# Moving the place of the split weights in SBUF: larger tiles with a start that steps by 64 bytes, one raw buffer fewer

## The chip, the core and the metric

The kernel runs on one core of one Trainium2 chip, and the time is device microseconds of one execution. Three executions of the kernel before gave 1087.91, 1085.91 and 1089.38 us, so the median is 1087.91 us. A fourth execution was taken with the hardware profiler, and all rows below are from it.

## What is computed

Two layers of a hybrid block over 256 positions of width 1024, in float32. In each layer a normed input goes through one wide projection, whose columns feed three things: an attention that picks 64 keys per query with an index score, a state-space scan (with a causal convolution ahead of it and a grouped norm behind it), and two gates. The two branches are projected, gated, added, and projected once more. Then comes a feed-forward layer with a short convolution.

```python
def reference(x, ...):
    for l in range(DEPTH):
        h = rms_norm(x, norm_mix_w[l])
        x = x + hybrid_mixer(h, w_in[l], ...)
        h = rms_norm(x, norm_ffn_w[l])
        x = x + conv_glu_ffn(h, ffn_w_up[l], ...)
    return rms_norm(x, norm_final_w)

def hybrid_mixer(h, w_in, ...):
    proj = h @ w_in
    ...
    a = dsa_attention(q, k, v, qi, ki, wi)
    b = mamba2_branch(z, xbc, dt_raw, ...)
    merged = jax.nn.sigmoid(g_attn) * (a @ w_proj_attn) + jax.nn.sigmoid(g_ssd) * (b @ w_proj_ssd)
    return merged @ w_out

def conv_glu_ffn(h, w_up, conv_w, conv_b, w_down):
    u = causal_dwconv(h @ w_up, conv_w, conv_b)
    gate, val = u[..., :FFN_DIM], u[..., FFN_DIM:]
    return (jax.nn.silu(gate) * val) @ w_down
```

## The kernel before

**Chunks.** All weights come in 350 chunks of at most 128 partitions by 1024 float32 (512 KB). SyncE loads a chunk into one of `RAW_BUFS` = 5 tiles `raw` (L174). ScalarE rounds it to the type of TensorE's faster float32 product, `whi` (L199), and VectorE writes what is left over, `wlo = raw - whi` (L200). There are three pairs `whi`, `wlo` (`SPLIT_BUFS`). Some chunks are split early into tiles of activations that are not in use then; these are the tables `EARLY_FFN`, `EARLY_MIX` and `EARLY_CONV`, and the tiles are called `ebig`, `ehxh`, `ex`, `es`, `ez` and so on. `take` (L188) hands the split pair of the next chunk to the caller, and loads and splits ahead as far as buffers allow. A raw tile comes free when VectorE's subtraction has read it.

**Products.** Each activation is split in the same way, into a high and a low part. A chunk of 8 blocks of 128 x 128 takes 24 matmuls: for each block the weights' high part times the activation's high part (L370) and low part (L371), and then for each block the low part of the weights times the activation's high part (L376). The block of weights is the stationary operand, which a LDWEIGHTS reads from SBUF (512 bytes of each partition), and the activation is the moving operand (256 columns, 1024 bytes of each partition). `n_outer` does this for one output tile, `k_outer` for four at a time. L370, L371 and L376 have 2464 matmuls each, 7392 together. The first projection's index and query columns (L549 to L551) go the other way round: the activation is stationary and 308 or 512 columns of weights are moving.

```python
        for j, k in enumerate(ks):
            nc.tensor.matmul(ps, wh[:, j, :], hi(k), start=first and j == 0, stop=False)
            nc.tensor.matmul(ps, wh[:, j, :], lo(k), start=False, stop=False)
```

**Order.** Attention, scan and norms are generators in three lanes. `take` runs a step of them after a chunk. The order of the instructions on each engine is set by a scheduler that simulates a timeline, with loads and splits at high priority; so the count of raw tiles has a say in where it puts the other work.

**Places.** Tiles lie in SBUF in the order in which their pools meet them, so a tile's start is the sum of the widths ahead of it. Matmul operands step by 512 or 1024 bytes inside a tile, so the start of each, modulo 512 bytes, is that of its tile:

| tiles | start modulo 512, before |
|---|---|
| `raw`, `whi`, `wlo` | 64 |
| `uh`, `ul` (tags Bm, Cm, lg0, lg1), `bL` and `ebig` (tags big0, big1) | 64 |
| tags s0 to s3: `bH`, `es`, and the first two pairs of `fH`, `fL` | 384 |
| `hxh`, `hxl`, `mH`, `mL`, `ths`, tags x0 to x3, z0 to z3 (`aH`, `aL`, the other `fH`, `fL`, `ex`, `ez`) | 0 |

The step from 64 to 384 comes from `wd`, which is 320 bytes wide, and the step to 0 from `dec`, which is 128. I call the start of the weights' block minus the start of the activation, modulo 512, the **distance** of a matmul. In the program before, the 7392 matmuls of L370, L371 and L376 have these distances: 64 for 5808 of them (`hxh`, `hxl`, `mH`, `aH`, later `fH`, with `whi` and `wlo`), 192 for 896 (`bH`, first `fH` and `fL`), 448 for 288 and 320 for 96 (`uh` and `ul` with early chunks), 0 for 304 (`bL`, and `hxh` with an early chunk in `ex`).

Of the kernel before, what the change touches and what calls it, by code (L numbers as in the profile page):

```python
# [9 lines left out]
F32 = mybir.dt.float32  # L10
F32R = mybir.dt.float32r
# [7 lines left out]
P = 128  # L19
# [11 lines left out]
BIG = 1.0e30  # L31
TOPK = 64

RAW_BUFS = 5
SPLIT_BUFS = 3

FIRST_PAIRS = 4

# [24 lines left out]
def hybrid_kernel(ctx: ExitStack, tc: tile.TileContext, a: dict, out: bass.AP):  # L63
    nc = tc.nc

    const = ctx.enter_context(tc.tile_pool(name="const", bufs=1))
    wraw = ctx.enter_context(tc.tile_pool(name="wraw", bufs=RAW_BUFS))
    wsp = ctx.enter_context(tc.tile_pool(name="wsp", bufs=SPLIT_BUFS))
    act = ctx.enter_context(tc.tile_pool(name="act", bufs=1))
# [67 lines left out]
        make_early(base, EARLY_MIX)  # L137
        make_early(base + 20, EARLY_CONV)

    st = {"cur": 0, "prep": 0, "dma": 0, "now": 0, "mm": None}  # L140
    lanes = {"norm": [], "attn": [], "scan": []}

    def side(lane, gen, delay):
# [25 lines left out]
    def load_some():  # L169
        while st["dma"] < len(order) and st["dma"] < st["prep"] + RAW_BUFS:  # L170
            i = order[st["dma"]]
            src, b, c = chunks[i]
            r = wraw.tile([P, 8 * 128], F32, name="raw", tag="raw")
            nc.sync.dma_start(r[:, :b * c].rearrange("p (b c) -> p b c", b=b), src)  # L174
            raws[i] = r[:, :b * c]
            st["dma"] += 1

    def split_tiles(j):
        if j in early:
            t0, t1 = early[j]  # L180
            if t0 == t1:
                t = act.tile([P, 2, 8 * 128], F32R, name=f"e{t0}", tag=t0)
                return [t[:, 0], t[:, 1]]
            return [(tmp if t in ("Xt", "pT") else act).tile([P, 8 * 128], F32R, name=f"e{t}", tag=t, bufs=1)
                    for t in (t0, t1)]
        return [wsp.tile([P, 8 * 128], F32R, name=t, tag=t) for t in ("whi", "wlo")]

    def take():  # L188
        i = st["cur"]
        with tc.high_priority():  # L190
            load_some()
            while st["prep"] < len(order):
                j = order[st["prep"]]
                if j not in early and sum(k not in early for k in splits) == SPLIT_BUFS:
                    break
                src, b, c = chunks[j]
                hi, lo = (t[:, :b * c] for t in split_tiles(j))
                r = raws.pop(j)
                nc.scalar.copy(out=hi, in_=r)  # L199
                nc.vector.tensor_sub(lo, r, hi.bitcast(F32))  # L200
                splits[j] = [t.rearrange("p (b c) -> p b c", b=b) for t in (hi, lo)]
                st["prep"] += 1
                load_some()
        st["cur"] += 1
        if st["mm"] is not None:
            side_steps()
        return splits.pop(i)
# [197 lines left out]
    for l in range(L):  # L405

        tok = [act.tile([P, 8 * T], F32, name=f"big{t}", tag=f"big{t}")[:, :1856] for t in range(2)]
        V = [act.tile([P, T], F32, name=f"V{t}", tag=f"V{t}") for t in range(2)]
        wd = act.tile([P, 2, 40], F32, name="wd", tag="wd")

        def rotate(v, t, heads, dim, rot, o):
            h = rot // 2
# [83 lines left out]
        dA = act.tile([P, 2, 32], F32, name="dA", tag="dA")  # L496
        Pc = act.tile([P, 2, 32], F32, name="Pc", tag="Pc")
        nP = act.tile([P, 2, 32], F32, name="nP", tag="nP")
        dec = act.tile([P, 32], F32, name="dec", tag="dec")

        prd = dram.tile([32, 2, P], F32, name=f"prd{l}")

# [491 lines left out]
```

## Time and profile before

| | |
|---|---|
| median of three executions | 1087.91 us |
| their range | 1085.91 to 1089.38 us |
| the profiled execution's time | 1091.08 us |
| its span, first to last instruction | 1089.1 us |
| PE busy, LDWEIGHTS (PEld) busy | 1064.4 us (98%), 1026.2 us (94%) |
| VectorE, ScalarE, GpSimd busy | 877.9 us, 696.2 us, 66.5 us |
| mean granted TensorE clock, as a share of the full one | 0.997 |
| read from HBM | 189.26 MB, 175 GB/s over the span |

The span is what the instructions cover; the profiled execution's time is 2 us more. A matmul's recorded duration covers its way through the array and overlaps the next one's, so the time that it costs is read from start to start, which is called its pitch below, and not from its duration.

### The profile page before, as it was taken

The page shows a single profiled execution, that of the slowest core. Times are in us where ns is not written, and L with a number is a line of the kernel's source. Part 1 is how long each engine was busy: PE and PEld are TensorE (multiplying, and loading weights), DVE is VectorE, ACT ScalarE, POOL GpSimd, SP SyncE. Part 2 cuts the span into 40 slices and gives each one's busy share as a digit, 9 for nine tenths or more (in the row PEclk, how much of TensorE's full clock was granted, in tenths as well). Part 3 has the DMA queues.
Part 4 walks back from the last instruction along what each step waited for, and adds up shares of the span by engine and source line. Part 5 has one row for each costly group of instructions (what it writes and reads, how often), then busy time and mean ns, then how long its engine had stood idle before and what let it go on. Part 6 is the DMA issues. An engine that isn't in the chain of part 4 may idle for free.

```text
span 1089.1 us, 22471 instructions
## 1 busy us (share of the span) xinstructions
PE 1064.4 (98%) x8704; PEld 1026.2 (94%) x8704; DVE 877.9 (81%) x1755; ACT 696.2 (64%) x1285; POOL 66.5 (6%) x74
## 2 busy tenths in 40 slices
PE   6999999999999999998999999999999999999997
PEld 5789989999999999998997999999999999999997
DVE  6898988879877899885668999887887878888643
ACT  5658878647555576665555699865665556666552
POOL 3000000022000200000100000000310020000010
PEclk9999999999999999999999999999999999999999
DMA  7546444555677346666645654555567761666661
GB/s 266 183 148 213 151 147 156 161 169 175 194 233 251 117 122 195 194 199 211 183 134 176 224 155 139 164 172 155 175 190 216 246 216 45 182 187 191 180 182 48
DMA packets 52841, 191.82 MB, mean 176 GB/s; under 512 B 5952, under 2 KB 6240, under 8 KB 51712
## 3 DMA queue, kind: packets, MB, share of 16 engines
q1 hardware_dynamic: 50832, 180.31, 53.8%
q0 software_dynamic: 1472, 9.17, 2.3%
q8 instruction: 68, 1.11, 0.4%
q10 hardware_dynamic: 432, 0.92, 0.2%
q14 instruction: 37, 0.30, 0.1%
HBM read 189.26 MB, written 1.11 MB: 175 GB/s over the span
## 4 chain that ended last, share of the span: by engine, by line
PE 85%; DMA 5%; ACT 4%; DVE 3%; issue 2%; DVEq 0%; ACTq 0%; POOLq 0%
PE acc L370 23%; PE acc L371 23%; PE acc L376 23%; PE acc L550 3%; PE acc L551 2%; PE acc L549 2%; DMA bc<-prd 2%; DMA raw<-in_wu_dram 2%; PE sb L705 1%; DVE wlo L200 1%; ACT whi L199 1%; PE sa L461 1%; DVE ul L327 1%; PE sa L589 1%; PE sa L614 1%
## 5 line engine op out<-in xcount | busy, mean ns | idle before, releaser
L199 ACT CAST whi<-raw 128x1024 fp32r<-128x1024 f32 (+2 forms) x320 | 331.9, 1040 | 225.1 <-PE acc L371 168.7
L200 DVE TENSOR_TENSOR wlo<-raw,whi 128x1024 fp32r<-128x1024 f32 (+2 forms) x320 | 387.0, 1212 | 107.5 <-ACT whi L199 103.1
L370 PE MATMUL acc<-hxh,whi 128*128 128x256 f32 x1456 | 353.3, 282 | 1.0 <-ACT ths L657 0.9
L371 PE MATMUL acc<-hxl,whi 128*128 128x256 f32 x1456 | 351.2, 281 | 0.0
L370 PEld LDWEIGHTS acc<-hxh,whi 128*128 128x128 f32 x1456 | 274.6, 189 | 2.7 <-issue 1.1
L371 PEld LDWEIGHTS acc<-hxl,whi 128*128 128x128 f32 x1456 | 274.7, 189 | 2.2 <-issue 1.9
L376 PE MATMUL acc<-hxh,wlo 128*128 128x256 f32 x1456 | 202.2, 280 | 0.0
L376 PEld LDWEIGHTS acc<-hxh,wlo 128*128 128x128 f32 x1456 | 183.0, 189 | 0.7 <-issue 0.7
L370 PE MATMUL acc<-fH,whi 128*128 128x256 f32 x352 | 84.6, 280 | 2.8 <-DVE xT L833 2.8
L371 PE MATMUL acc<-fL,whi 128*128 128x256 f32 x352 | 84.4, 280 | 0.0
L649 DVE SCALAR_TENSOR_TENSOR cv<-acc,half,cv 128x255 f32<-128x255 f32 (+2 forms) x144 | 67.1, 474 | 3.9 <-ACT cv L647 3.4
L370 PEld LDWEIGHTS acc<-fH,whi 128*128 128x128 f32 x352 | 66.6, 190 | 3.1 <-issue 3.0
L851 DVE SCALAR_TENSOR_TENSOR cv<-acc,small,cv 128x255 f32<-128x255 f32 (+1 forms) x144 | 68.4, 477 | 1.3
L371 PEld LDWEIGHTS acc<-fL,whi 128*128 128x128 f32 x352 | 66.6, 189 | 0.0
L370 PE MATMUL acc<-bH,whi 128*128 128x256 f32 x256 | 62.4, 280 | 0.1
L371 PE MATMUL acc<-bL,whi 128*128 128x256 f32 x256 | 62.3, 282 | 0.0
L337 POOL TENSOR_TENSOR ssq<-ssq,sq 128x256 f32<-128x256 f32 x30 | 27.1, 904 | 516.8 <-ACT sq L333 516.2
L549 PE MATMUL acc<-whi,uh 128*128 128x512 f32 (+1 forms) x112 | 42.0, 392 | 9.2 <-ACT whi L199 9.2
L376 PE MATMUL acc<-fH,wlo 128*128 128x256 f32 x352 | 50.1, 281 | 0.0
L370 PEld LDWEIGHTS acc<-bH,whi 128*128 128x128 f32 x256 | 48.1, 188 | 0.4 <-issue 0.4
L371 PEld LDWEIGHTS acc<-bL,whi 128*128 128x128 f32 x256 | 48.2, 188 | 0.0
L695 ACT ACTIVATE bc<-bc,nP 128x128 f32<-128x128 f32 x128 | 39.9, 390 | 11.6 <-DMA bc<-prd 11.5
(281 smaller groups left out, 1873.0 us busy)
## 6 DMA issues: line engine op xcount, KB each, us to landing
raw<-in_wu_dram SPq DMA_DIRECT2D x88, 512.0 KB, 3.6
raw<-in_wx_dram SPq DMA_DIRECT2D x48, 512.0 KB, 3.6
raw<-in_wd_dram SPq DMA_DIRECT2D x38, 512.0 KB, 3.7
raw<-in_wz_dram SPq DMA_DIRECT2D x32, 512.0 KB, 3.6
raw<-in_wp_dram SPq DMA_DIRECT2D x32, 512.0 KB, 4.4
raw<-in_wq_dram SPq DMA_DIRECT2D x24, 512.0 KB, 4.5
raw<-in_wgs_dram SPq DMA_DIRECT2D x16, 512.0 KB, 3.6
bc<-prd POOLq DMA_DIRECT2D x8, 1024.0 KB, 7.3
```

Source lines behind the costliest of these rows:

```text
L199: nc.scalar.copy(out=hi, in_=r)
L200: nc.vector.tensor_sub(lo, r, hi.bitcast(F32))
L337: nc.gpsimd.tensor_add(self.acc, self.acc, sq)
L370: nc.tensor.matmul(ps, wh[:, j, :], hi(k), start=first and j == 0, stop=False)
L371: nc.tensor.matmul(ps, wh[:, j, :], lo(k), start=False, stop=False)
L376: st["mm"] = nc.tensor.matmul(ps, wl[:, j, :], hi(k), start=False, stop=last and j == len(ks) - 1)
L549: nc.tensor.matmul(pss[t], nrm.hi(k)[:, s], wh[:, kk, :], start=f, stop=False)
L550: nc.tensor.matmul(pss[t], nrm.hi(k)[:, s], wl[:, kk, :], start=False, stop=False)
L551: st["mm"] = nc.tensor.matmul(pss[t], nrm.lo(k)[:, s], wh[:, kk, :], start=False, stop=e)
L649: nc.vector.scalar_tensor_tensor(v[:, j:], ps[:, :T - j], cw(l, 3 - j, i), v[:, j:], op0=OP.mult, op1=OP.add)
L695: nc.scalar.activation(E[:, h, :], E[:, h, :], AF.Relu, bias=nP[:, c, 8 * g + h:8 * g + h + 1])
L851: nc.vector.scalar_tensor_tensor(v[:, j:], uu[:, :T - j], fw(l, 2 - j, i), v[:, j:], op0=OP.mult, op1=OP.add)
```

## The change

Split weights get tiles of 9 x 128 instead of 8 x 128 columns, and the chunk lies in such a tile from column `first` on, which moves on by 16 columns (64 bytes) after every `GROUP` = 8 pairs and starts anew after eight such steps. To make room, one of the five raw tiles goes. `wd` is padded from 320 to 448 bytes and `dec` from 128 to 512, which puts the tags s0 to s3 at 0 modulo 512 and leaves all that was at 0 there. `uh`, `ul` and `big` stay at 64.

```diff
-RAW_BUFS = 5
+RAW_BUFS = 4
 SPLIT_BUFS = 3
+
+GROUP = 8
...
-    st = {"cur": 0, "prep": 0, "dma": 0, "now": 0, "mm": None}
+    st = {"cur": 0, "prep": 0, "dma": 0, "now": 0, "mm": None, "turn": 0}
...
-        return [wsp.tile([P, 8 * 128], F32R, name=t, tag=t) for t in ("whi", "wlo")]
+        first = 16 * ((st["turn"] // GROUP) % 8)
+        st["turn"] += 1
+        return [wsp.tile([P, 9 * 128], F32R, name=t, tag=t)[:, first:first + 8 * 128] for t in ("whi", "wlo")]
...
-        wd = act.tile([P, 2, 40], F32, name="wd", tag="wd")
+        wd = act.tile([P, 112], F32, name="wd", tag="wd")[:, :80].rearrange("p (a b) -> p a b", a=2)
...
-        dec = act.tile([P, 32], F32, name="dec", tag="dec")
+        dec = act.tile([P, 128], F32, name="dec", tag="dec")[:, :32]
```

In the changed program the 7392 matmuls are spread over eight distances: 0 for 950, 64 for 792, 128 for 856, 192 for 930, 256 for 902, 320 for 792, 384 for 856, 448 for 1314. No instruction is added or removed. The padding and the moving start leave the order of all engines as it is; the fourth raw tile's absence alone makes the scheduler put some of the work of the lanes elsewhere, in the two mixers, on PE, VectorE and ScalarE. Lines of the changed kernel are 4 higher than before from `take` on. Two places:

TensorE, first layer, behind the last chunk of the index columns. L298 (L302 in the changed kernel) are the two matmuls that spread the norm's factor over the partitions; the rest are query products. Before:

```order
L551 MATMUL acc<-eXt,ul_105 128x308
L298 MATMUL sb<-dg,ones 128x256
L549 MATMUL acc<-whi,uh_102 128x512
L550 MATMUL acc<-wlo,uh_102 128x512
L551 MATMUL acc<-whi,ul_104 128x512
L549 MATMUL acc<-whi,uh_102 128x512
L298 MATMUL sb<-dg,ones 128x256
```

Of the change:

```order
L554 MATMUL acc<-wlo,uh_102 128x512
L555 MATMUL acc<-whi,ul_104 128x512
L553 MATMUL acc<-whi,uh_102 128x512
L554 MATMUL acc<-wlo,uh_102 128x512
L555 MATMUL acc<-whi,ul_104 128x512
L553 MATMUL acc<-whi,uh_102 128x512
L302 MATMUL sb<-dg,ones 128x256
```

Four products of 512 columns stood between the two; in the changed program there are 13.

ScalarE, just behind it: the factor's row `rrow`, the rounding of the normed activation `hxh`, and the next splits (`ex` is an early chunk). Before:

```order
L300 COPY rrow<-sb 128x256
L347 CAST hxh<-ht 128x256 x3
L199 CAST ex_530<-raw 128x1024
L512 ACTIVATE u<-u 128x64
L347 CAST hxh<-ht 128x256
L199 CAST whi<-raw 128x1024
```

Of the change:

```order
L304 COPY rrow<-sb 128x256
L351 CAST hxh<-ht 128x256
L203 CAST whi<-raw 128x1024
L351 CAST hxh<-ht 128x256 x2
L203 CAST whi<-raw 128x1024
L351 CAST hxh<-ht 128x256
L445 COPY qiT<-sa 128x4x128
L448 COPY kk_149<-sa 128x128
L203 CAST whi<-raw 128x1024
L203 CAST ex_528<-raw 128x1024
```

The early chunk `ex` is rounded three splits later.

## Rows read from the trace of the kernel before

**Rows 1.** The page: busy time by engine, and the chain that ended last

```profile
PE 1064.4 (98%) x8704; PEld 1026.2 (94%) x8704; DVE 877.9 (81%) x1755; ACT 696.2 (64%) x1285; POOL 66.5 (6%) x74
...
PE 85%; DMA 5%; ACT 4%; DVE 3%; issue 2%; DVEq 0%; ACTq 0%; POOLq 0%
```

**Rows 2.** Waits: engine, line waited for, us in total, times, longest

```profile
ACT whi L199 <- PE acc L371: 168.7, 143, 5.4
...
PE acc L549 <- ACT whi L199: 9.2, 1, 9.2
...
PE acc L370 <- DVE xT L833: 4.4, 4, 2.8
```

**Rows 3.** Stretches: us, each engine's busy us (and instructions), clock, DMA share, GB/s

```profile
390.00:480.00 90.00, 90.00 (x797) 90.00 (x796) 82.33 (x138) 62.11 (x103) 0.00 (x0) 1.00 0.63 190
...
920.00:1010.00 90.00, 90.00 (x766) 90.00 (x765) 78.90 (x133) 60.37 (x98) 0.00 (x0) 1.00 0.63 186
```

**Rows 4.** Line L376: count, duration ns least/median/most, first and last start us

```profile
L376 PE MATMUL acc<-hxh,wlo x1456: 276/281/469, 73.2 to 1017.2; 128*128 128x256 f32 x182
...
L376 PE MATMUL acc<-bH,wlo x256: 276/280/284, 293.9 to 867.9; 128*128 128x256 f32 x128
...
L376 PE MATMUL acc<-aH,wlo x128: 276/276/388, 198.3 to 822.0; 128*128 128x256 f32 x128
...
L376 PE MATMUL acc<-mH,wlo x128: 281/281/283, 339.8 to 890.9; 128*128 128x256 f32 x128
...
L376 PE MATMUL acc<-hxh,ex x16: 281/283/283, 91.7 to 624.9; 128*128 128x256 f32 x16
```

**Rows 5.** Stretches at distance 192 (first two) and 448 (last two)

```profile
484.50:494.50 10.00, 10.00 (x87) 10.00 (x86) 6.24 (x8) 4.01 (x6) 0.00 (x0) 1.00 0.46 137
...
1018.00:1028.00 10.00, 10.00 (x87) 10.00 (x86) 6.11 (x8) 4.03 (x7) 0.00 (x0) 1.00 0.44 135
...
376.50:385.50 9.00, 9.00 (x78) 9.00 (x78) 8.90 (x26) 5.65 (x12) 0.00 (x0) 1.00 0.01 3
905.50:914.50 9.00, 9.00 (x82) 9.00 (x81) 9.00 (x26) 6.01 (x13) 0.00 (x0) 1.00 0.00 0
```

**Rows 6.** PE in order of time, distance 0: start us, us, operation, count

```profile
89.76 0.28 PE L370 MATMUL acc<-hxh,ex 128*128 128x256 f32 x1
...
91.68 1.12 PE L376 MATMUL acc<-hxh,ex 128*128 128x256 f32 x8
```

**Rows 7.** L549, weights moving: least/median/most ns, `ebig` at distance 0, `eths` not

```profile
L549 PE MATMUL acc<-ebig,uh x16: 301/303/387, 14.8 to 556.4; 128*128 128x308 f32 x16
...
L549 PE MATMUL acc<-eths,uh x8: 301/303/305, 24.1 to 561.8; 128*128 128x308 f32 x8
```

**Rows 8.** One chunk in steady state, VectorE, SyncE and ScalarE, and the load's landing

```profile
399.97 1.23 DVE L200 TENSOR_TENSOR wlo<-raw,whi 128x1024 fp32r<-128x1024 f32 x1
...
401.23 13.93 SPq L174 DMA_DIRECT2D raw<-in_wu_dram  x6
...
409.76 1.05 ACT L199 CAST whi<-raw 128x1024 fp32r<-128x1024 f32 x1 [0.59 <-PE acc L371]
412.48 1.05 ACT L199 CAST whi<-raw 128x1024 fp32r<-128x1024 f32 x1 [0.89 <-PE acc L371]
...
raw<-in_wu_dram SPq DMA_DIRECT2D x88, 512.0 KB, 3.6
```

**Rows 9.** The start: early index chunks on VectorE and TensorE, and their load

```profile
15.23 2.06 DVE L200 TENSOR_TENSOR ebig<-raw,ebig 128x616 fp32r<-128x616 f32 x2
...
24.12 0.30 PE L549 MATMUL acc<-eths,uh 128*128 128x308 f32 x1
...
raw<-in_wi_dram SPq DMA_DIRECT2D x16, 308.0 KB, 4.1
```

**Rows 10.** Tile `ex`: its split, and its first reader

```profile
L370 PEld LDWEIGHTS acc<-hxh,ex x16: 187/192/192, 89.6 to 623.7; 128*128 128x128 f32 x16
...
L199 ACT CAST ex<-raw x6: 1047/1048/1050, 33.5 to 854.6; 128x1024 fp32r<-128x1024 f32 x6
```

## The prediction

> **What bounds the kernel now.** I read the page first, for the busy shares and the chain that ended last. PE is busy for 98% of the span and holds 85% of the chain [rows 1]; VectorE, the next, is at 81%. The waits say the same: what PE itself waits for is small, 9.2 us once for the first split and 4.4 us in all for residuals, while ScalarE waits 143 times, 168.7 us in all, for PE to free a `whi` tile [rows 2]. So loads and splits run ahead, and time can only come from the pitch of the matmuls, from PE standing still, or from a load that becomes late.
>
> Next I cut out stretches, because the mean hides two pitches. Both stretches of [rows 3] are the feed-forward layer, the same chunks, tiles and distance (64), at the full clock. In the first layer 796 weight loads fit into 90 us, in the second 765. With up to two records that lap over an edge left out, the pitches are 113.3 and 117.6 ns (I use 117.7). So one distance allows two pitches, a short and a long one, and a pitch once taken holds over hundreds of matmuls. The duration tells which one a tile's matmuls had [rows 4]: 276 ns goes with the short pitch, 279 to 281 with the long one. `aH` has its median at 276 and `mH` at 281 though both lie at distance 64, and the 1456 matmuls of `hxh` have theirs at 281: more than half have the long pitch. I take 4 in 10 with the short one, which makes a mean pitch of 0.4 x 113.3 + 0.6 x 117.7 = 115.9 ns at distance 64.
>
> Then I looked for distances where it is not like this. At 192 both layers show 85 or 86 loads in 10 us, 117.7 ns [rows 5]; at 448 one layer has about 77 in 9 us, the other 80 to 81, so both pitches again [rows 5]. At 0 the 16 matmuls from 89.76 to 91.68 us come every 120 ns [rows 6], and their durations are 283 ns with hardly any spread [rows 4]. So the distance has a say: 0 and 192 know only long pitches, 64 and 448 know both.
>
> **The change, part by part.**
>
> *Places.* Matmuls of L370, L371 and L376 by distance, times the pitches above (320 is taken like 64 and 448; its 96 matmuls hardly count before):
> Before: 6192 at 64, 320 and 448 x 115.9 = 717.7 us; 896 at 192 x 117.7 = 105.5; 304 at 0 x 120 = 36.5. Sum 859.6 us.
> After: 2898 at 64, 320 and 448 x 115.9 = 335.9; 930 at 192 x 117.7 = 109.5; 950 at 0 x 120 = 114.0. The distances 128 (856), 256 (902) and 384 (856) do not occur before. I take each from its two neighbours: 128 and 256 lie between a mixed and a long one, 116.8 ns, and 384 between two mixed ones, 115.9. That is 100.0 + 105.4 + 99.2 = 304.6. Sum 864.0 us, which is 4.4 us more. The bulk of it is the 950 matmuls moved to distance 0, 950 x (120 - 115.9) = 3.9 us.
> Bounds: had all three unseen distances the short pitch, their 2614 matmuls would take 296.2 us, and the change of the sum is -4.0; were they all like distance 0, 313.7 us, and it is +13.5. The coin of the mixed distances moves 2898 matmuls between 113.3 and 117.7, by -7.5 to +5.2 us, since which pitch a stretch falls into can't be read ahead of time.
>
> [...]
>
> *Products with moving weights* (L549 to L551). Their distances change too. With 308 columns `ebig`, at distance 0, and `eths`, which is not, have the same median, 303 ns [rows 7]. I take 0.
>
> *The fifth raw tile.* In steady state VectorE's subtraction ends at 401.20 us and SyncE issues the load that takes over its tile at 401.23 [rows 8]. It lands 3.6 us later, at 404.8. With five tiles that is the chunk rounded at 412.48; with four it would be the one at 409.76, which still leaves 4.9 us. At the start it is closest: with four tiles the load into `eths` waits for the first of the two `ebig` subtractions, about 16.6 us, lands 4.1 us later, and needs 0.7 + 0.8 us for its splits, so 22.2 us; PE reads it at 24.12 [rows 9]. The work that hides it is 1.9 us of index products. I take 0, with at most 2 us were that cover gone. SyncE's order is unchanged, and nothing else waits in its queue.
>
> *Moved instructions.* The second factor matmul comes nine products of 512 columns later, about 2 us, on its way to `rrow` and `hxh`; PE first multiplies `hxh` by a low part at 73.2 us [rows 4], over 40 us later. `ex`, rounded behind three more splits of 1.05 us, is first rounded at 33.5 and first read at 89.6 us [rows 10]. Both are hidden. Where the lanes' matmuls fall elsewhere in the mixers, PE may stand still a little more or less; the waits of [rows 2] suggest a few us in all, so 0, within 3 either way.
>
> Sum: +4.4 us. The profiled execution took 1091.08 us, its span 1089.1; the sum makes its time 1095.5. It ran 3.2 us above the median of 1087.91, so against the median I expect 1087.91 + 4.4 = 1092.3, say **1092 us**. With the bounds of the unseen distances and some luck of the mixed ones its own range is 1088 to 1101.
>
> **The rivals.**
>
> *Faster: the unseen distances have only the short pitch, and hand it on.* A pitch lasts until something breaks it [rows 3]. If 256 and 384 allow only 113.3, PE may enter 320 and 448 at the short pitch and keep it there until 0 comes. That is -4.0 (all three unseen ones), and 2106 matmuls at 320 and 448 x (113.3 - 115.9) = -5.5: -9.5 us, 1078 us. It decides from the point where the unseen distances run below 115.1 ns on average (there the sum is 0, with the mixed ones as they were). For it: 6 of 10 matmuls have the long pitch now, and a place that moves gives a long stretch of it like that of the second layer's feed-forward an end. Against it: two of the five distances seen have long pitches only, and one of them, 192, is a neighbour of 128 and 256.
>
> *No change: the distance plays no part.* [...] For it: both pitches at one distance, with identical instructions [rows 3]. Against it: 192 is long in both layers [rows 5], 0 in both [rows 4].
>
> *Slower by the loads.* Were four raw tiles too few in the bursts of early chunks, PE would wait for splits; 2 us at the start and as much again in the second layer, 1092 to 1096 with the first term. [rows 8] leave 4.9 us of room, so I count it with the forecast's upper end.
>
> **How the numbers follow.** A measurement of this kernel can tell about 0.3% (3.3 us) from no change. The forecast (all eight distances in equal turns) gets 0.43 and lies above that; the faster rival 0.33; no change 0.24. The predicted time is the forecast's. Eight in ten: I reach down to the faster rival's 1078 with a little left over, 1077, and up to the bound of +13.5, 1101. Below lie only the cases where nearly all matmuls have the short pitch, above those where the unseen distances are as bad as 0 and the coins fall badly too.
>
> **What would show it.** The matmuls of the two feed-forward layers change their pitch every 192 matmuls (eight chunks of 24) if distance matters, to 120 ns at distance 0 and 117.7 at 192; a pitch that runs on through a step would speak for the third case. Distances 128, 256 and 384 show their pitch for the first time: below 115.1 on average makes the forecast wrong. ScalarE's waits for `raw` should grow in the bursts and PE's should not.

## The result, and the profile after

The changed kernel is slower: a median of 1098.61 us over four executions (1095.70 to 1098.84), against 1086.91 us of the kernel before on the same chip (four, 1085.08 to 1089.38). The ratio on record is 1.0091, with a 95% interval from 1.0066 to 1.0116, so about 10 us; the two medians alone differ by 11.7. The profiled execution was the fastest of the four (1095.70 us, span 1093.9), and that of before, 1091.08 us, lay above its median. So the spans of the two traces differ by 4.8 us only, and the sum below accounts for these.

The page of the changed kernel: busy time by engine, and the chain that ended last, to hold against [rows 1].

```profile
PE 1071.1 (98%) x8704; PEld 1034.9 (95%) x8704; DVE 879.6 (80%) x1755; ACT 698.6 (64%) x1285; POOL 67.0 (6%) x74
...
PE 88%; DMA 4%; ACT 3%; DVE 3%; issue 2%; DVEq 0%; ACTq 0%; POOLq 0%
```

The same 8704 matmuls keep PE busy for 6.7 us longer, and PE holds 88% of the chain instead of 85%. VectorE, ScalarE and GpSimd are busy for 2.4 us more at most. The waits of the changed kernel (engine, line waited for, us in total, times, longest):

```profile
ACT whi L203 <- PE acc L375: 178.4, 154, 5.5
...
PE acc L553 <- ACT whi L203: 9.1, 1, 9.1
PE acc L374 <- DVE ths L821: 2.3, 2, 1.2
...
PE acc L374 <- DVE xT L837: 1.4, 1, 1.4
...
ACT ex L203 <- DMA raw<-in_wu_dram: 6.0, 4, 2.5
...
ACT es L203 <- DMA raw<-in_wu_dram: 3.6, 4, 1.3
```

ScalarE waits 178.4 us for PE to free a `whi` tile, 9.7 more than in [rows 2]. Of PE's own waits the first stays (9.1 us against 9.2), those for residuals (`xT`) fall from 4.4 to 1.4, and those for `ths` grow from 0.9 to 2.3; all that are listed come to 15.1 us against 16.8. So PE was not made to wait; it needs longer for each matmul. Stretches of the changed kernel show where (us, busy us and instructions of PE, PEld, DVE, ACT, POOL, clock, DMA share, GB/s). They answer to [rows 3] and [rows 5]. The first two are the first layer's feed-forward at distance 64 and 256, the other seven the second layer's at 128, 192, 256, 320, 384, 448 and 0.

```profile
461.00:481.00 20.00, 20.00 (x172) 20.00 (x171) 17.16 (x29) 13.31 (x23) 0.00 (x0) 1.00 0.61 190
...
531.00:551.00 20.00, 20.00 (x168) 20.00 (x168) 9.19 (x14) 8.98 (x13) 1.72 (x2) 1.00 0.61 171
...
929.00:949.00 20.00, 20.00 (x171) 20.00 (x170) 17.94 (x32) 13.54 (x23) 0.00 (x0) 1.00 0.65 190
951.50:971.50 20.00, 20.00 (x172) 20.00 (x172) 17.16 (x29) 13.29 (x22) 0.00 (x0) 1.00 0.64 190
974.50:994.50 20.00, 20.00 (x169) 20.00 (x168) 16.81 (x29) 13.21 (x21) 0.00 (x0) 1.00 0.63 183
997.00:1017.00 20.00, 20.00 (x179) 20.00 (x178) 17.86 (x30) 13.23 (x23) 0.00 (x0) 1.00 0.67 199
1019.00:1039.00 20.00, 20.00 (x171) 20.00 (x170) 11.36 (x15) 8.64 (x11) 0.00 (x0) 1.00 0.60 190
1042.00:1062.00 20.00, 20.00 (x171) 19.92 (x170) 10.07 (x13) 10.46 (x17) 3.35 (x4) 1.00 0.58 170
1064.00:1084.00 20.00, 20.00 (x169) 20.00 (x169) 6.78 (x9) 6.45 (x9) 1.61 (x2) 1.00 0.19 55
```

PE is busy throughout and the clock is full in each, yet 20 us hold 178 weight loads at 320, 172 at 192, 171 at 64 in the first layer, 170 at 128 and 384, and 168 or 169 at 256 and 0. (At 448 two short stops lie inside.) The count steps where the place steps, after 192 matmuls.

To have a pitch for each distance I took the differences of successive starts of L374, L375 and L380 (L370, L371 and L376 before), left out those above 130 ns, which are stops, and sorted the rest by the operands' places in the program. A matmul is called short below when its pitch is at most 114 ns. Means in ns, with the number of matmuls at that distance:

| distance | 0 | 64 | 128 | 192 | 256 | 320 | 384 | 448 | all |
|---|---|---|---|---|---|---|---|---|---|
| before | 119.3 (304) | 115.9 (5808) | | 117.6 (896) | | 115.8 (96) | | 115.4 (288) | 116.23 |
| after | 119.8 (950) | 116.3 (792) | 118.6 (856) | 117.6 (930) | 119.7 (902) | 115.6 (792) | 118.6 (856) | 116.9 (1314) | 117.89 |
| forecast | 120 | 115.9 | 116.8 | 117.7 | 116.8 | 115.9 | 115.9 | 115.9 | |

0 reads like 256, 64 like 320, 128 like 384. At 448 a third of the matmuls have activations that start at 64; the 890 others have 117.2, near the 117.6 of 192. So the pattern repeats every 256 bytes, not every 512.

Durations of L380 in the changed kernel answer to [rows 4] (count, least/median/most, first and last start):

```profile
L380 PE MATMUL acc<-hxh,wlo x1456: 274/281/469, 69.5 to 1020.8; 128*128 128x256 f32 x182
...
L380 PE MATMUL acc<-aH,wlo x128: 276/280/393, 194.6 to 825.9; 128*128 128x256 f32 x128
L380 PE MATMUL acc<-mH,wlo x128: 276/278/283, 338.6 to 895.5; 128*128 128x256 f32 x128
```

`aH` went from 276 to 280 ns and `mH` from 281 to 278. `hxh` keeps its median, although its mix of pitches changed, so the median of a duration is a coarse witness. These medians, 278 to 281 ns, are over twice the mean pitch of 117.89, so the records of successive matmuls overlap; what a duration covers beyond the pitch no run shows. The first and last starts of `hxh` say more: 3.7 us earlier than before in the first layer, 3.6 us later at the end.

### The profile page after: what moved, and what is told of

It reads as the page before. It is cut to its first block, busy times and chain, and to the rows that moved or that the text cites. A ratio compares the mean times of both kernels' runs of the same rounds, so it can differ in the third digit from the quotient of the medians.

```text
span 1093.9 us, 22464 instructions
## 1 busy us (share of the span) xinstructions
PE 1071.1 (98%) x8704; PEld 1034.9 (95%) x8704; DVE 879.6 (80%) x1755; ACT 698.6 (64%) x1285; POOL 67.0 (6%) x74
## 4 chain that ended last, share of the span: by engine, by line
PE 88%; DMA 4%; ACT 3%; DVE 3%; issue 2%; DVEq 0%; ACTq 0%; POOLq 0%
PE acc L374 24%; PE acc L375 24%; PE acc L380 24%; PE acc L553 3%; PE acc L554 3%; PE acc L555 3%; DMA bc<-prd 1%; ACT whi L203 1%; PE sb L709 1%; ACT bc L699 1%; DVE wlo L204 1%; DMA raw<-in_wu_dram 1%; PE sa L593 1%; DMA raw<-in_wi_dram 1%; PE sa L465 1%
## 5 line engine op out<-in xcount | busy, mean ns | idle before, releaser
L203 ACT CAST whi<-raw 128x1024 fp32r<-128x1024 f32 (+2 forms) x320 | 331.7, 1038 | 242.4 <-PE acc L375 178.4
L374 PE MATMUL acc<-hxh,whi 128*128 128x256 f32 x1456 | 359.3, 284 | 0.0
L375 PE MATMUL acc<-hxl,whi 128*128 128x256 f32 x1456 | 356.9, 283 | 0.0
L375 PEld LDWEIGHTS acc<-hxl,whi 128*128 128x128 f32 x1456 | 275.1, 189 | 2.2 <-issue 1.9
L374 PEld LDWEIGHTS acc<-hxh,whi 128*128 128x128 f32 x1456 | 275.0, 189 | 1.4 <-issue 1.2
L380 PE MATMUL acc<-hxh,wlo 128*128 128x256 f32 x1456 | 204.6, 282 | 0.0
L380 PEld LDWEIGHTS acc<-hxh,wlo 128*128 128x128 f32 x1456 | 185.4, 189 | 0.6 <-issue 0.5
L374 PE MATMUL acc<-fH,whi 128*128 128x256 f32 x352 | 86.0, 282 | 1.4 <-DVE xT L837 1.4
L375 PE MATMUL acc<-fL,whi 128*128 128x256 f32 x352 | 85.9, 281 | 0.0
L374 PEld LDWEIGHTS acc<-fH,whi 128*128 128x128 f32 x352 | 66.3, 189 | 1.7 <-ACT whi L203 1.6
L375 PEld LDWEIGHTS acc<-fL,whi 128*128 128x128 f32 x352 | 66.3, 189 | 0.0
L374 PE MATMUL acc<-bH,whi 128*128 128x256 f32 x256 | 62.0, 281 | 2.3 <-DVE ths L821 2.3
L375 PE MATMUL acc<-bL,whi 128*128 128x256 f32 x256 | 61.9, 280 | 0.0
L374 PEld LDWEIGHTS acc<-bH,whi 128*128 128x128 f32 x256 | 48.2, 188 | 2.6 <-ACT whi L203 2.6
L380 PE MATMUL acc<-fH,wlo 128*128 128x256 f32 x352 | 50.4, 281 | 0.0
L375 PEld LDWEIGHTS acc<-bL,whi 128*128 128x128 f32 x256 | 48.2, 188 | 0.0
```

Source lines behind the costliest of these rows:

```text
L380: st["mm"] = nc.tensor.matmul(ps, wl[:, j, :], hi(k), start=False, stop=last and j == len(ks) - 1)
```

## The experiments

Four theories stood at the start. **D**, distance: the distance sets the pitch, and the new distances are worse on average. **R**, raw tile and order: the missing fifth tile and the shifted work of the lanes cost the time. **M**, moving: a start that steps breaks a good pitch, whatever the places are. **K**, kick: PE falls into one of two pitches by chance, and a short disturbance gives it another throw, which could be used. The texts on the last runs add **A**, that 88 is a distance at which only the short pitch lasts, and **B**, that 64, 76 and 88 are alike. All ratios are to the kernel before on the same chip (medians 1088.55, 1087.98 and 1088.18 us in the three sets), with 95% intervals.

### r4: the fourth raw tile alone

```diff
-RAW_BUFS = 5
+RAW_BUFS = 4
```

> The kernel before with four raw tiles and nothing else, so it has the order of the changed kernel and the places of the kernel before. Theory D (distance: the changed kernel lost by the distances that its matmuls run at, and the raw tile and the moved work cost nothing): no slower than before, ratio 0.997 to 1.003, about 1084 to 1090 us; the other work of the lanes may even gain, since matmul starts outside L370, L371, L376 and L549 to L551 covered 4.2 us less in the changed trace. Rival R (the missing raw tile and the order cost it): most of the loss is here, ratio 1.006 to 1.012.

Measured: 1086.64 us, ratio 0.9981 (0.9961 to 1.0002). The page, and L376:

```profile
PE 1061.0 (98%) x8704; PEld 1025.6 (94%) x8704; DVE 879.2 (81%) x1755; ACT 697.6 (64%) x1285; POOL 66.3 (6%) x74
```

```profile
L376 PE MATMUL acc<-hxh,wlo x1456: 276/281/469, 68.9 to 1014.7; 128*128 128x256 f32 x182
```

This kernel has the changed order of all engines and the old places. R falls: it is not slower than before, and its mean pitch is that of before, 116.28 ns against 116.23. The first `hxh` product starts at 68.9 us as against 73.2, so the earlier start seen in the changed kernel comes with the fourth tile's order. Every engine has the same order of instructions in r4 as in the changed kernel, so the two differ in places alone: by the ratios 1.0091 / 0.9981, 1.1% or about 12 us, and by the mean pitches of the two traces 7392 x (117.89 - 116.28) ns = 11.9 us.

### fix64 and fix0: the start stands still

Everything of the change stays, but the start is constant, so that nearly all matmuls have distance 64 (6704 of them), or 0 (6752).

```diff
-        first = 16 * ((st["turn"] // GROUP) % 8)
+        first = 0
```

```diff
-        first = 16 * ((st["turn"] // GROUP) % 8)
+        first = 16 * 7
```

> The changed kernel with the start of the split weights held at its first place: distance 64 for all matmuls of hxh, mH, aH, fH, bH. Theory D: pitch 115.9 ns on average where the changed kernel had 117.9 in its trace, so 7264 x 2.0 ns = 14.5 us less than the changed kernel, and less than before by the 896 matmuls that leave 192 (1.6 us): about 1082 to 1088 us, ratio 0.995 to 1.001, with both pitches, 113.3 and 117.7 ns, in the trace. Rival R: like the changed kernel, 1.006 to 1.012, since raw tiles and order are the same. Rival M (the moving itself costs, whatever the places): gains as in D, so this run alone does not tell D from M.

> The changed kernel with the start held at its last place, distance 0 for hxh, mH, aH, fH, bH (and 192 modulo 256 for uh, ul and bL). Theory D: nearly 7000 matmuls at 119.75 ns instead of 116.2 on average before, so 24 us more than before less the 4 us of the order: 1103 to 1112 us, ratio 1.015 to 1.024, and hardly any pitch of 113 ns. Rival M: a start that stands still costs nothing, ratio 0.997 to 1.003. Rival R: as the changed kernel, 1.006 to 1.012.

Measured: fix64 1085.18 us, ratio 0.9965 (0.9942 to 0.9988); fix0 1108.25 us, ratio 1.0184 (1.0160 to 1.0208). Stretches of the feed-forward layers, first fix64, then fix0:

```profile
440.00:460.00 20.00, 20.00 (x178) 20.00 (x178) 17.92 (x30) 13.35 (x23) 0.00 (x0) 1.00 0.67 198
930.00:950.00 20.00, 20.00 (x179) 20.00 (x178) 18.07 (x32) 14.06 (x24) 0.00 (x0) 1.00 0.67 193
```

```profile
440.00:460.00 20.00, 20.00 (x169) 20.00 (x168) 17.02 (x30) 13.04 (x22) 0.00 (x0) 1.00 0.62 185
...
940.00:960.00 20.00, 20.00 (x169) 20.00 (x168) 17.66 (x30) 13.03 (x23) 0.00 (x0) 1.00 0.61 183
```

The two differ in one number in the source, and in nothing that an engine is told to do. 178 loads against 168 in the same time, both at full clock, with PE never idle. Over all matmuls at the held distance the mean pitch is 115.26 ns at 64 (56% short) and 119.78 at 0 (1% short). D is shown: the place alone makes 23 us.

### move256: a start that moves by 256 bytes

```diff
-        first = 16 * ((st["turn"] // GROUP) % 8)
+        first = 64 * ((st["turn"] // GROUP) % 2)
```

> The changed kernel with a start that moves between two places 256 bytes apart after every eight pairs, so it moves as often, but the distance modulo 256 is 64 all the time. Theory D (period 256): as with the start held at 64, ratio 0.994 to 1.001, about 1082 to 1089 us, pitch mean 115 to 116 ns. Rival M (moving costs at each step): up to the changed kernel's 1.007 to 1.012.

Measured: 1081.80 us, ratio 0.9951 (0.9931 to 0.9972). Stretches over four places each, both layers:

```profile
390.00:470.00 80.00, 80.00 (x709) 80.00 (x707) 72.50 (x122) 54.04 (x91) 0.00 (x0) 1.00 0.67 196
920.00:1000.00 80.00, 80.00 (x708) 80.00 (x708) 72.50 (x122) 54.08 (x90) 0.00 (x0) 1.00 0.65 195
```

With the record left out that laps over an edge, 706 loads in 80 us are 113.3 ns: the short pitch runs on through every step of the place in these stretches. M falls, and a shift by 256 bytes is no shift for the pitch (mean 115.05 ns, against fix64's 115.26).

### map16 and map4: the distance in finer steps

map16 steps through 16 places 16 bytes apart, map4 through 16 places 4 bytes apart, from distance 36 to 96. Each was executed once.

```diff
-        first = 16 * ((st["turn"] // GROUP) % 8)
+        first = 4 * ((st["turn"] // GROUP) % 16)
```

```diff
-        first = 16 * ((st["turn"] // GROUP) % 8)
+        first = 57 + (st["turn"] // GROUP) % 16
```

> The changed kernel with steps of 16 bytes over sixteen places, so that the trace shows the pitch at every distance of 16 bytes within 256, some 450 matmuls each. Theory D with a period of 256 bytes: 64 mixed at 113.3 and 117.7, 128 at 118.6, 192 at 117.2, 0 at 119.75, as in the changed kernel, and the ones in between not above 120; what the steps of 16 bytes between them show is open, and any distance that has the short pitch alone would be the place to hold. Rival M: the pitch does not follow the distance, and each step costs some matmuls at its seam. About 1085 to 1105 us.

> The changed kernel with steps of 4 bytes over sixteen places, distances 36 to 96, to see how wide the good place around 64 is. If a line of SBUF of 16 bytes or more is what counts, some neighbours of 64 (60 to 76, or 64 to 76) run like 64, at 113.3 or mixed; if the exact distance counts, only 64 has a pitch below 115 ns. 1085 to 1103 us, near the upper end in the second case.

Measured: 1098.69 and 1097.35 us. Stretches of map16 at distance 48, 64 and 80:

```profile
440.00:460.00 20.00, 20.00 (x173) 20.00 (x172) 17.17 (x29) 13.11 (x22) 0.00 (x0) 1.00 0.61 189
463.00:481.00 18.00, 18.00 (x161) 18.00 (x160) 15.89 (x29) 12.16 (x20) 0.00 (x0) 1.00 0.62 186
485.00:505.00 20.00, 20.00 (x170) 20.00 (x170) 13.69 (x18) 9.94 (x13) 0.00 (x0) 1.00 0.64 198
```

and of map4 at distance 88, 36, 40 and 52:

```profile
395.00:415.00 20.00, 20.00 (x179) 20.00 (x178) 18.69 (x33) 13.51 (x23) 0.00 (x0) 1.00 0.67 193
462.00:482.00 20.00, 20.00 (x169) 20.00 (x169) 16.80 (x29) 13.05 (x22) 0.00 (x0) 1.00 0.62 187
485.00:505.00 20.00, 20.00 (x171) 20.00 (x170) 13.32 (x19) 10.28 (x14) 0.00 (x0) 1.00 0.64 196
...
1000.00:1020.00 20.00, 20.00 (x179) 20.00 (x178) 17.83 (x31) 12.89 (x23) 0.00 (x0) 1.00 0.67 196
```

In map16 distance 64 (modulo 256) is alone: 113.45 ns, 98% short. At 112 and 240 18% are short, and the means of all 15 others lie between 117.5 and 120.0. In map4 the means are

| distance | 36 | 40 | 44 | 48 | 52 | 56 | 60 | 64 | 68 | 72 | 76 | 80 | 84 | 88 | 92 | 96 |
|---|---|---|---|---|---|---|---|---|---|---|---|---|---|---|---|---|
| ns | 119.9 | 119.2 | 117.9 | 118.2 | **114.3** | 117.7 | 118.4 | **115.5** | 118.4 | 118.2 | **115.0** | 118.8 | 120.0 | **114.1** | 118.3 | 119.0 |

Four distances, 12 bytes apart, allow the short pitch for over half of their matmuls; 4 bytes beside each of them the mean is 117.7 ns or more. So a distance does not resemble its neighbours, by which I had guessed the unseen ones.

### kick: one pair in eight at another place

```diff
-        first = 16 * ((st["turn"] // GROUP) % 8)
+        first = 60 if st["turn"] % GROUP == 0 else 64
```

> Distance 64 held, but one pair in eight lies at distance 48, which holds no pitch for long. In the trace with steps of 16 bytes, all 384 matmuls at 64 that came behind 48 ran at the short pitch. Theory K (leaving the place for one chunk throws PE out of the long pitch): share of the short pitch at distance 64 up from 56% to 75% or more, mean there 114.5 or less; the 832 matmuls at 48 cost 832 x (117.6 - 115.3) = 1.9 us, the others gain 5872 x 0.8 = 4.7 us, so 1080 to 1085 us, ratio 0.992 to 0.997. Rival (the pitch is set anew at each stop of PE by how the lanes' work breaks in, and the kick only adds its own price): 0.997 to 1.001, with the share unchanged.

Measured: 1084.88 us, ratio 0.9973 (0.9956 to 0.9989), not to be told from fix64's 0.9965. 64% of the matmuls at 64 were short (mean 114.93 ns), and those at 48 had 118.04. K is not borne out: there is no gain over fix64. The short share at 64 is larger (64% against 56%), but this is one trace of each kernel, and the 832 disturbed matmuls are slower.

### all64: every matmul at distance 64

The kernel before with four raw tiles, and paddings (two more, of `xT` and `rot`, are left out below) that put all 7392 matmuls at 64, those with early chunks too.

```diff
-                t = act.tile([P, 2, 8 * 128], F32R, name=f"e{t0}", tag=t0)
-                return [t[:, 0], t[:, 1]]
...
+                o = 16 if t0 == "ths" else 0
+                t = act.tile([P, 2 * 8 * 128 + 4 * o], F32R, name=f"e{t0}", tag=t0)[:, o:o + 2 * 8 * 128]
+                return [t[:, :8 * 128], t[:, 8 * 128:]]
+            o = 0 if t0 == "hxh" or t0 == "hxl" else 16
...
-        wd = act.tile([P, 2, 40], F32, name="wd", tag="wd")
+        wd = act.tile([P, 128], F32, name="wd", tag="wd")[:, :80].rearrange("p (a b) -> p a b", a=2)
...
-        dec = act.tile([P, 32], F32, name="dec", tag="dec")
+        dec = act.tile([P, 64], F32, name="dec", tag="dec")[:, :32]
```

> A version of my own with four raw tiles: every one of the 7392 matmuls at distance 64, the early chunks and bL too (tiles padded, early chunks 64 bytes into wider tiles), and a start that stands still. Theory D: the 688 matmuls that ran at 0 or 192 with the start held at 64 gain 117.4 - 115.3 = 2.1 ns each, 1.4 us; about 1081 to 1087 us, ratio 0.993 to 0.999, no matmul pitch of 120 outside seams. If the mixed pitch falls the long way more often, up to 1.001.

Measured: 1081.14 us, ratio 0.9946 (0.9926 to 0.9966), mean pitch 114.87 ns, 66% short. Its twelve executions spread from 1077.81 to 1088.32 us.

### hold88, hold52, hold76, hold100: one distance held

As all64, with the split pairs in tiles of 8 x 128 + 64 columns from a constant column on (6, 61, 3, 9), and the early chunks moved likewise; 7200 matmuls lie at the distance of the name, 192 at 0. hold76:

```diff
-        return [wsp.tile([P, 8 * 128], F32R, name=t, tag=t) for t in ("whi", "wlo")]
+        return [wsp.tile([P, 8 * 128 + 64], F32R, name=t, tag=t)[:, 3:3 + 8 * 128] for t in ("whi", "wlo")]
```

> Four raw tiles, distance 88 held for 7200 of the 7392 matmuls (the other 192, early chunks in z0 to z3, ths, Xt and pT, lie at 0). In the trace with steps of 4 bytes, 84% of the matmuls at 88 had the short pitch, and after each stop of PE they came back to it within some ten matmuls; at 64 a stop leaves PE at 113.3 or at 117.7 and it stays there. Theory A (88 has the short pitch as the only one that holds): mean pitch 113.8 to 114.4 against 114.9 with all at 64, 4 to 8 us less than that run: 1072 to 1079 us, ratio 0.986 to 0.992. Rival B (64, 76, 88 are alike and the shares seen there were luck): 0.993 to 0.999, a mixed pitch with stretches of 117.7.

> The same with distance 52, which had 81% at the short pitch, but one stretch behind a stop that stayed on a pattern of 117 to 120 ns. Theory A: between 88 and 64, mean 114.2 to 115.2, ratio 0.989 to 0.997, 1075 to 1084 us. Rival B: as at 64, 0.993 to 0.999.

> The same with distance 76 (68% short, with stretches of 117.7 in between like at 64). Both theories: as all at 64, mean 114.5 to 115.5, ratio 0.993 to 0.999, 1081 to 1087 us.

> The same with distance 100, not seen by 4 bytes. The distances that have the short pitch lie 12 bytes apart: 52, 64, 76, 88; 112 had 18% of it, and 96 and 92 none. If the ladder of 12 bytes goes on, 100 has the short pitch for most of its matmuls: mean below 115, ratio 0.986 to 0.997. If it ends at 88, the mean is 117.5 to 120 as at 92, 96 or 112 and the ratio 1.005 to 1.020.

| | median us | ratio (95%) | mean pitch there, ns | short |
|---|---|---|---|---|
| hold52 | 1081.53 | 0.9944 (0.9931 to 0.9958) | 114.70 | 76% |
| hold76 | 1076.07 | 0.9894 (0.9879 to 0.9910) | 113.77 | 92% |
| hold88 | 1085.34 | 0.9973 (0.9959 to 0.9988) | 115.18 | 50% |
| hold100 | 1110.89 | 1.0215 (1.0201 to 1.0230) | 119.90 | 0% |

Both feed-forward layers of hold76, and its busy time:

```profile
PE 1047.0 (97%) x8704; PEld 1011.1 (94%) x8704; DVE 877.8 (82%) x1755; ACT 695.9 (65%) x1285; POOL 66.3 (6%) x74
```

```profile
385.00:475.00 90.00, 90.00 (x797) 90.00 (x796) 81.54 (x137) 61.63 (x102) 0.00 (x0) 1.00 0.64 191
910.00:1000.00 90.00, 90.00 (x797) 90.00 (x796) 81.97 (x138) 61.90 (x104) 0.00 (x0) 1.00 0.64 190
```

and of hold100:

```profile
400.00:490.00 90.00, 90.00 (x752) 90.00 (x752) 76.47 (x127) 59.62 (x97) 0.00 (x0) 1.00 0.61 182
935.00:1025.00 90.00, 90.00 (x752) 90.00 (x751) 77.52 (x130) 59.98 (x99) 0.00 (x0) 1.00 0.62 179
```

hold76 has in both layers the 796 loads that [rows 3] show in one of them only. It is 1.06% faster than the kernel before, better than its expectation. hold88, which had the largest share in map4 (84% short), kept the short pitch for half of its matmuls only, so A fell for 88; B fell too, since 76 is clear of 64 and 88. The share that a distance had over a few hundred matmuls of map4 didn't say what it would have in the whole program. And the ladder of 12 bytes ends: the next rung, 100, is as bad as 0. 34.8 us lie between hold76 and hold100, which differ only in the place of tiles, 24 bytes apart.

## Why the prediction was right, and where it was off

The forecast was 1092 us, slower, within 1077 to 1101. The measured 1098.61 us is inside, on the forecast side, but the shift, 10 us by the ratio and 11.7 by the medians, is over twice the 4.4 us that I had worked out. That the spans of the two traces differ by 4.8 us, nearly the forecast's sum, is chance: it comes of a larger term and two that I had put at 0.

*What bounds the kernel.* Right. The pitch of the matmuls decides. hold76, which has the order of r4 and other places only, has a span of 1074.8 us against r4's 1085.9. But a pitch does not reach the span in full, which the sum had not considered: hold76's is 2.35 ns less than r4's on average, 17.4 us over 7392 matmuls, and the stops between them (what starts over 130 ns apart take beyond the mean pitch) grew from 22.9 to 28.7 us. In the changed kernel they shrank to 18.3.

*Two pitches at one distance, and none at 0 and 192.* Right: 0 had 119.8 and 192 117.6 ns, as [rows 5, 6] say. So was the step from [rows 4] to 4 in 10 short at distance 64: sorted by place, before had 43%, and a mean of 115.9 ns. The term that I called the bulk, the matmuls moved to distance 0, held as well: 119.8 ns against 120.

*Places: the unseen distances.* This is the term that was mis-sized. I took 128 and 256 at 116.8 and 384 at 115.9 from their neighbours; they have 118.6, 119.7 and 118.6. That is 856 x 1.8 + 902 x 2.9 + 856 x 2.7 ns = 6.5 us more. The mixed distances add 1.3 us, by 448: I had read it off 288 matmuls with early chunks, which were mixed [rows 5], and it is short in 22% only (15% where the activation starts at 0). The step that failed is the interpolation: I had assumed a pitch that runs smoothly, modulo 512. It repeats after 256 bytes, and between 64 and its neighbours on either side it differs by 2.9 ns within 4 bytes (115.5 and 118.4 in map4).

*The sum.* With the measured pitches the term becomes about +12 us (7392 x 1.66 ns). In the two traces, the times from each start of these matmuls to the next, stops included, add up to 879.7 us before and 889.7 after, +10.0, since the stops got 2.3 us shorter. Those of the products with moving weights went from 100.4 to 99.5, those of the lanes' matmuls from 92.0 to 87.9. 10.0 - 0.9 - 4.1 = 5.0, and the spans differ by 4.8; the rest lies ahead of the first matmul and behind the last.

*Products with moving weights, the fifth raw tile.* Both near 0, as taken: the products have 0.9 us less, and r4, which lacks the fifth tile, is at 0.9981.

*Moved instructions.* I gave 0 within 3 us; the traces show 4.1 us less from the lanes' matmuls. By r4 the order is worth between 4 us and nothing.

*What would show it.* The pitch does change every 192 matmuls. The unseen distances lie above 115.1, so the faster rival fell. (The sum is 0 at 114.8 ns, (304.6 - 4.4) / 2614, and not at 115.1; it changes nothing here.) ScalarE's waits for `raw` did not grow as I had said: 39.9 us in 31 waits after, 54.1 in 25 before. That sign was wrong, at no cost, since PE's waits did not grow either.

*The rivals.* "No change" fell by fix64 against fix0, which differ by 2%, and by hold76 against hold100, which differ by 3%: a matmul of 256 columns with a weight load of its own took 115.3 ns on average in one and 119.8 in the other of the first pair, 113.8 and 119.9 in the second, by the place of the tiles alone. What makes the place count no run shows. "Slower by the loads" fell by r4 (0.9981).

**What stays open.** Why the pattern has 256 bytes and rungs of 12, and why one distance allows two pitches, no run shows. Distances off the grid of 16 bytes were tried from 36 to 96 only, so there may be better ones than 76. Whether the activation's own start counts beside the distance wasn't tried apart: matmuls whose activation starts at 64 differ by up to 3 ns from those at 0 with the same distance, but they are few and alternate with other distances. At distance 192 two pairs of places can be held against each other, activations at 384 with weights at 64 (before, 484.5 to 494.5 us) and at 0 with weights at 192 (changed, 951.5 to 971.5 us): both have 117.8 ns.

## What to carry to other kernels

Where matmuls follow each other without a gap, compare the pitch from start to start with the best stretch of the same instructions: a spread at full clock and with no waits can come from where the operands lie in SBUF (here 115.3 ns in fix64 and 119.8 in fix0). Then hold a distance and scan it in steps of 4 bytes, over the whole program; don't interpolate, and don't rotate through all places, which buys an average of good and bad ones (117.9 ns in the changed kernel, 113.8 in hold76). Expect a part of the gain to be lost to longer stops (in hold76 5.8 of 17.4 us). Every padding and every buffer ahead of a tile moves its start, so an edit that "only" changes a width can move the time: here by between -1.1% and +2.2%.

## What the runs showed of the hardware

- The same 24 matmuls of a chunk, at full clock, take 113.3 to 120 ns each, by the distance between the starts of stationary and moving operand modulo 256 bytes: 119.9 ns held at 100, 113.8 held at 76.
- Steps of 4 bytes matter: in map4 114.3 ns at 52, 117.7 at 56.
- At distance 64 PE settles at 113.3 or 117.7 ns after a stop or a step of the distance, and stays there. In the trace of the kernel before, 56 stretches of 24 matmuls or more at 64 run without a break; behind their first dozen 33 keep the long pitch to their end, 23 the short one, and none changes. In the changed kernel PE came from distance 0 into the stretch at 461 us, and 191 of 192 matmuls there had the long pitch; at 320 in the second layer 190 of 192 had the short one.
- At 76, in hold76, up to seven matmuls at the start of such a stretch have 115 to 125 ns, and then the pitch is 113.3, in 45 of 48 stretches; three stay at 120.
- The time varies from execution to execution by 10.5 us in all64 (twelve), 3.0 in hold76 (four) and 0.7 in hold52 (five). One execution of each kernel was traced, so no trace shows that the two pitches make this spread.
- In the trace of the kernel before, products of 512 columns in the rounded type (L549 to L551) that follow each other start 227 ns apart in the median, and the plain float32 ones of L735, also of 512 columns, 428 to 534 ns.
